# The begin of a decoder layer's kernel, rebuilt: S5 constants beside the input's arrival, S5 input tiles in pairs, another order of the halves

## The chip, the cores and the metric

The kernel runs on one core of one Trainium2 chip. The metric is the device time of one launch in microseconds, as the median of several runs. The engines are named as in the profile: PE (matrix multiplication; PEld is its weight load), DVE (VectorE), ACT (ScalarE), POOL (GpSimd) and SP (which here issues DMAs only).

## The reference, cut to what matters

One layer of a hybrid decoder on x (1024 tokens, 1024 channels), in float32. What the change touches is the first norm, the columns of the input projection that feed the S5 branch, and the numbers that the S5 branch derives from its parameters.

```python
h = rms_norm(x, norm_mix_pre[l])
proj = h @ w_in[l]                       # columns: RWKV-7 | S5 input u | two gates
u_s5 = proj[..., N_RWKV_COLS:N_RWKV_COLS + S5_WIDTH]      # 512 columns
...
lam = lax.complex(a_re, a_im)
dt = jnp.exp(log_step)[:, None]
a_bar = jnp.exp(lam * dt)
b_bar = ((a_bar - 1.0) / lam)[..., None] * lax.complex(b_re, b_im)
bu = jnp.einsum('gpc,blgc->blgp', b_bar, ug)
_, states = lax.associative_scan(s5_combine, (a_elems, bu), axis=1)
y = jnp.real(jnp.einsum('gcp,blgp->blgc', c, states)) + d * ug
```

RWKV-7 time mixing, the two gates, the output projection and a gated MLP follow.

## The kernel before, in words

Channels lie on the partitions, tokens along the free dimension, in two halves of 512 tokens. Each matmul operand is split into a high part, which ACT rounds to the matmul's format, and a low part, the rest, which DVE (for x: DVE and POOL in turn) subtracts. A product of two such operands is three matmuls (`mm3_steps`: high by high, low by high, high by low), so a tile of 128 columns by 512 tokens over the 8 blocks of 128 channels is 24 matmuls into one PSUM bank (`gm`).

The begin, up to the first tile of `mix_in` (the RWKV columns of the projection):

- `load_x` loads eight x tiles of a half. `setup` loads the constants (`csts`: an identity, masks, a row of numbers) and small vectors (`vecs`), and makes a few derived vectors on DVE.
- `norm` squares x on ACT, adds pairs on DVE, sums over channels with small matmuls on PE (`sumsq`, into `chk`), makes the reciprocal root with small dependent DVE instructions (`rstd`), spreads it over the partitions with PE (`spread`), copies that to SBUF (`rbc`), multiplies each x tile with it on DVE and splits the result into `hh` and `hl`.
- `s5_in` makes the four tiles of S5 input. Its weights come through `load_w`: an SP load into `wf` (two buffers), high part `wh` on ACT, low part `wl` on DVE (four buffers each). It takes tiles 0 and 1 over both halves, then 2 and 3; each result goes to DRAM (`US`) and comes back reordered (`u8`).
- `s5_setup` makes the S5 constants from the parameters: some 115 DVE instructions on 128 x 32 numbers, with sines on ACT.
- From then on two lanes run for each of four batches of eight S5 groups: `s5_tables` (tables on DVE, sines on ACT) and `s5_batch` (the rotation, the scan and the output).

PE's instructions stand in the order in which the code emits them. On the other engines a scheduler orders them by the priority under which they were emitted (`HPN` above `HPW` above `HP`). The emission order comes from `drive`: lanes yield their costs and due times, and between them work is taken from the list `self.fill`. In the kernel before, S5 input tiles are such fill work, half 1's norm is a lane, and `s5_setup` is emitted behind it at the lower priority `HP`:

```python
self.fill = [self.s5_in((0, 1)), self.s5_in((2, 3)), self.mix_in()] + ...
self.drive([(HPN, self.norm(1, xs[1], xp))])
with tc.high_priority(HP):
    self.s5_setup()
```

## Time and profile before

| | us |
|---|---|
| median of 3 runs (1638.65 to 1644.3) | 1640.43 |
| profiled execution | 1641.32 |
| its span, first to last instruction | 1639.5 |
| PE busy, of the span | 1513.2 (92%) |
| DVE busy | 1161.2 (71%) |
| ACT busy | 718.6 (44%) |
| POOL busy | 177.9 (11%) |
| first matmul of the S5 input tiles | 26.14 |
| first eviction of mix_in | 102.57 |

The profiled execution is one run; the difference between its time and its span lies around the first and the last instruction. Matmuls overlap, so a row shows 0.39 us for one that starts 0.23 us after the one before; start to start is what counts. A row of a timeline gives the start, the busy time, engine, line, operation, output and inputs, and in brackets the idle time before and what ended it. The granted clock of TensorE is 1.00 at full speed.

### The profile page before, as it was taken

What the parts mean: (1) busy time and instruction counts of PE and PEld (TensorE: products, weight loads), DVE (VectorE), ACT (ScalarE), POOL (GpSimd) and SP (SyncE); (2) the same over time, 40 slices, a digit from 0 to 9 for tenths busy, and PEclk for the clock granted to TensorE, in tenths of its full rate; (3) what the DMA queues carried; (4) which work ended last, traced back from release to release, by engine and by line L of the source; (5) the groups of instructions that cost most, each with busy time, mean ns of one, the idle gap of its engine ahead of it and who ended that gap; (6) DMA issues with size and microseconds to landing.
All of it is one profiled execution on the core that took longest, in us unless ns stands there. A gap on an engine that the chain in (4) does not pass through costs nothing. (4 is left out here: it accounts for less than half of the span.)

```text
span 1639.5 us, 23417 instructions
## 1 busy us (share of the span) xinstructions
PE 1513.2 (92%) x8644; PEld 1206.2 (74%) x8644; DVE 1161.2 (71%) x2091; ACT 718.6 (44%) x1173; POOL 177.9 (11%) x260
## 2 busy tenths in 40 slices
PE   5899898999997997989987999999999999999995
PEld 4688787777675775656765778778888888788774
DVE  5898765657544578586478478977777777778767
ACT  4345543222353344346543444544445445443451
POOL 2100102232112024212020000000000000000000
PEclk9799999999997998999999999999999999999997
DMA  5255243443333166444256254322222224862622
GB/s 176 68 146 158 85 129 116 141 127 100 103 105 109 63 184 186 117 118 153 85 153 229 88 193 145 131 90 78 90 78 77 92 89 152 295 227 93 227 92 103
DMA packets 115811, 212.67 MB, mean 130 GB/s; under 512 B 22208, under 2 KB 28352, under 8 KB 115696
## 3 DMA queue, kind: packets, MB, share of 16 engines
q1 hardware_dynamic: 102672, 174.16, 33.5%
q0 software_dynamic: 11296, 32.82, 6.8%
q10 hardware_dynamic: 1728, 4.20, 0.7%
q8 instruction: 68, 1.11, 0.3%
q14 instruction: 47, 0.39, 0.1%
HBM read 156.07 MB, written 52.95 MB: 127 GB/s over the span
## 5 line engine op out<-in xcount | busy, mean ns | idle before, releaser
L173 PE MATMUL gm<-hh,wh 128*128 128x512 f32 x688 | 300.1, 436 | 21.7 <-DVE last L966 7.2
L174 PE MATMUL gm<-hl,wh 128*128 128x512 f32 x688 | 280.1, 407 | 7.7 <-DVE hl L228 4.7
L175 PE MATMUL gm<-hh,wl 128*128 128x512 f32 x688 | 277.6, 404 | 0.0
L158 DVE TENSOR_TENSOR wl<-wf,wh 128x512 fp32r<-128x512 f32 x179 | 125.1, 700 | 106.5 <-ACT wh L157 103.9
L157 ACT CAST wh<-wf 128x512 fp32r<-128x512 f32 x179 | 110.7, 619 | 185.2 <-PE gm L174 96.0
L173 PEld LDWEIGHTS gm<-hh,wh 128*128 128x128 f32 x688 | 134.3, 195 | 58.8 <-issue 10.3
L174 PEld LDWEIGHTS gm<-hl,wh 128*128 128x128 f32 x688 | 134.9, 196 | 36.1 <-DVE hl L228 8.2
L175 PEld LDWEIGHTS gm<-hh,wl 128*128 128x128 f32 x688 | 134.9, 196 | 29.5
L1562 PE MATMUL d<-xl,wh 128*128 128x512 f32 x308 | 120.3, 391 | 4.1 <-DVE xl L228 4.1
L1561 PE MATMUL d<-xh,wh 128*128 128x512 f32 x308 | 120.2, 390 | 2.0 <-DVE zg L1417 2.0
L1563 PE MATMUL d<-xh,wl 128*128 128x512 f32 x308 | 119.9, 389 | 0.0
L1387 PE MATMUL rp<-t,h 128*128 128x512 f32 x216 | 84.4, 391 | 2.4 <-ACT p L1401 1.7
L1389 PE MATMUL rp<-t,l 128*128 128x512 f32 x216 | 84.2, 390 | 0.5 <-DVE l L228 0.5
L1388 PE MATMUL rp<-t,h 128*128 128x512 f32 x216 | 84.1, 389 | 0.0
L1562 PEld LDWEIGHTS d<-xl,wh 128*128 128x128 f32 x308 | 57.8, 188 | 17.7 <-DVE xl L228 5.8
L1561 PEld LDWEIGHTS d<-xh,wh 128*128 128x128 f32 x308 | 57.8, 188 | 14.4 <-DVE zg L1417 2.4
L1563 PEld LDWEIGHTS d<-xh,wl 128*128 128x128 f32 x308 | 57.8, 188 | 11.8
L227 ACT CAST h<-r 128x1024 fp32r<-128x1024 f32 x34 | 35.8, 1054 | 61.1 <-PE rp L1388 29.6
L228 DVE TENSOR_TENSOR l<-r,h 128x1024 fp32r<-128x1024 f32 x34 | 41.6, 1225 | 29.3 <-ACT h L227 27.7
L1408 DVE SCALAR_TENSOR_TENSOR y<-zv,vecs,y 128x1023 f32<-128x1023 f32 (+1 forms) x36 | 46.1, 1281 | 8.6 <-ACT y L1406 8.6
L1387 PEld LDWEIGHTS rp<-t,h 128*128 128x128 f32 x216 | 40.5, 188 | 11.9 <-ACT p L1401 2.5
L1389 PEld LDWEIGHTS rp<-t,l 128*128 128x128 f32 x216 | 40.5, 188 | 9.5 <-DVE l L228 1.0
(450 smaller groups left out, 3408.9 us busy)
## 6 DMA issues: line engine op xcount, KB each, us to landing
r<-in_w_up_dram SPq DMA_DIRECT2D x36, 512.0 KB, 3.9
wf<-in_w_in_dram SPq DMA_DIRECT2D x68, 256.0 KB, 3.1
st<-in_w_down_dram SPq DMA_DIRECT2D x55, 256.0 KB, 4.3
st<-ACT SPq DMA_DIRECT2D x44, 256.0 KB, 4.5
wf<-in_w_up_dram SPq DMA_DIRECT2D x36, 256.0 KB, 2.9
ACT<-y POOLq DMA_DIRECT2D x18, 512.0 KB, 2.9
GT<-ev SPq DMA_DIRECT2D x32, 256.0 KB, 2.4
wf<-in_w_br_dram SPq DMA_DIRECT2D x32, 256.0 KB, 2.8
```

The lines of the kernel that those rows point to most:

```text
L157: nc.scalar.copy(h[:, :n], f[:, :n])
L158: nc.vector.tensor_tensor(l[:, :n], f[:, :n], h[:, :n].bitcast(F32), ALU.subtract)
L173: mm(ps, a, xh[k], start=k == 0, stop=False)
L174: mm(ps, a, xl[k], start=False, stop=False)
L175: mm(ps, b, xh[k], start=False, stop=k == n - 1)
L1387: mm(ps, wh[:, c], xh, start=first and k == 0, stop=False, skip_group_check=True)
L1388: mm(ps, wh[:, c], xl, start=False, stop=False, skip_group_check=True)
L1389: mm(ps, wl[:, c], xh, start=False, stop=k == 3, skip_group_check=True)
L1408: V.scalar_tensor_tensor(y[:, lag:], z[:, 0:1024 - lag], self.vec(nme, i), y[:, lag:], ALU.mult, ALU.add)
L1561: mm(ps, wh[:, c], xh[:, x], start=start, stop=False, skip_group_check=True)
L1562: mm(ps, wh[:, c], xl[:, x], start=False, stop=False, skip_group_check=True)
L1563: mm(ps, wl[:, c], xh[:, x], start=False, stop=stop, skip_group_check=True)
```

## The change

All of it lies ahead of `mix_in`.

- `setup` loads only the identity of `csts`. The other 608 KB are loaded on SP behind x, and so are the S5 parameters b and c of the first two batches. The three small S5 parameters that `s5_setup` begins with are loaded on ACT's queue instead of SP's.
- A new function `start` writes the order out by hand. `s5_setup` is emitted right behind half 0's norm, at a priority just under the norm's (`HPN - 50000`).
- `s5_in` takes two tiles at once: for each block of channels three matmuls of one tile and then three of the other. The order is tiles 2 and 3 of half 0, tiles 0 and 1 of half 0 (with half 1's norm between the steps), tiles 0 and 1 of half 1, and, as fill work, tiles 2 and 3 of half 1 (`s5_rest`). The weights of tiles 2 and 3 are loaded and split twice.
- In `norm`, all low parts are on DVE; the spread is read from PSUM, without the copy to SBUF; squares have eight buffers instead of four.
- `T_TAB0`, the due time of the first tables behind their start, is 18 instead of 38.

```diff
-        nc.gpsimd.dma_start(self.csts[:, 128:NCST], self.a["cst"][:, 128:NCST])
...
-            nc.sync.dma_start(ls, a["s5_ls"])
-            nc.sync.dma_start(lr, a["s5_a"][0])
-            nc.sync.dma_start(li, a["s5_a"][1])
+            nc.scalar.dma_start(ls, a["s5_ls"])
+            nc.scalar.dma_start(lr, a["s5_a"][0])
+            nc.scalar.dma_start(li, a["s5_a"][1])
...
-        self.spread(bc, self.rstd(ss, 1e-6, 1.0 / D))
-        rbc = pool.tile([128, 512], F32, tag="rbc", name=self.nm("rbc"), bufs=1)
-        nc.scalar.copy(rbc, bc)
+        self.spread(bc, y)
         h = []
         for k in range(NK):
-            nc.vector.scalar_tensor_tensor(xs[k], xs[k], self.vec("g_mix_pre", k), rbc, ALU.mult, ALU.mult)
-            h.append(self.hsplit(xs[k], k, self.hp[th], eng=nc.gpsimd if k % 2 else nc.vector))
+            nc.vector.scalar_tensor_tensor(xs[k], xs[k], self.vec("g_mix_pre", k), bc, ALU.mult, ALU.mult)
+            h.append(self.hsplit(xs[k], k, self.hp[th]))
...
-    def s5_in(self, bs):
...
+    def s5_in(self, bs, th, ws):
+
+        xh, xl = [h[0] for h in self.h[th]], [h[1] for h in self.h[th]]
+        ps = [self.gmp() for _ in bs]
+        for _ in zip(*(self.mm3_steps(p, w, 0, xh, xl) for p, w in zip(ps, ws))):
+            yield 1.36
+        for b, p in zip(bs, ps):
+            y = self.ev((128, 8, 64))
+            self.nc.scalar.copy(y.rearrange("p i n -> p n i"), p.rearrange("p (n j) -> p n j", j=8)[:, :, ::-1])
+            self.nc.sync.dma_start(self.US[b].rearrange("i c g n -> (c g) i n")[:, :, th * 64:th * 64 + 64], y)
...
+    def start(self, xp):
...
+        with tc.high_priority(HPN):
+            xs = [self.load_x(0, xp)]
+            self.setup()
+            norms = [self.norm(0, xs[0], xp)]
+        with tc.high_priority(HPW):
+            ws = [self.s5_ws((2, 3))]
+        go(norms[0], 6)
+        with tc.high_priority(HPW):
+            xs.append(self.load_x(1, xp))
+            norms.append(self.norm(1, xs[1], xp))
+        with tc.high_priority(HPN - 50000):
+            self.s5_setup()
+        with tc.high_priority(HP):
+            self.nc.sync.dma_start(self.csts[:, 128:NCST], self.a["cst"][:, 128:NCST])
+            self.s5w = {}
+            self.s5_load(0)
+            self.s5_load(1)
+        a = self.s5_in((2, 3), 0, ws[0])
+        go(a, 8)
+        with tc.high_priority(HPW):
+            ws.append(self.s5_ws((0, 1)))
+        go(a)
+        b = self.s5_in((0, 1), 0, ws[1])
+        go(b)
+        for _ in range(4):
+            go(norms[1])
+            go(b)
+        go(norms[1])
+        go(b, 1)
+        go(norms[1])
+        go(b, 3)
+        c = self.s5_in((0, 1), 1, ws[1])
+        go(c, 9)
+        for b in range(2):
+            self.load_u8(b)
+
+    def s5_rest(self):
+
+        yield from self.s5_in((2, 3), 1, self.s5_ws((2, 3)))
+        yield 0
+        self.load_u8(2)
+        self.stored = 3
...
-T_US, T_TAB0, T_TAB, T_TRIG, T_SCAN = 5.0, 38.0, 20.0, 12.0, 13.0
+T_US, T_TAB0, T_TAB, T_TRIG, T_SCAN = 5.0, 18.0, 20.0, 12.0, 13.0
```

The scheduler moves more than the diff tells. On DVE, half 0's reciprocal root (`rv` is the scaled sum of squares, `rsy` and `rsh` the steps of the root) was a run of its own before:

```order
L266 TENSOR_SCALAR rv_279<-chk_241 128x4
L137 TENSOR_SCALAR rsy_281<-rv_279 128x4
L138 TENSOR_SCALAR rsy_281<-rsy_281 128x4
L140 TENSOR_TENSOR rsh_282<-rsy_281 128x4
L141 SCALAR_TENSOR_TENSOR rsh_282<-rsh_282,rv_279 128x4
```

With the change, S5 constants (`sm`) stand between its steps, two after each:

```order
L266 TENSOR_SCALAR rv_285<-chk_248 128x4
L333 SCALAR_TENSOR_TENSOR sm_432<-sm_430,sm_422 128x32
L333 SCALAR_TENSOR_TENSOR sm_472<-sm_460,sm_470 128x32
L137 TENSOR_SCALAR rsy_287<-rv_285 128x4
L333 SCALAR_TENSOR_TENSOR sm_434<-sm_432,sm_422 128x32
L328 TENSOR_TENSOR sm_474<-sm_466,sm_472 128x32
L138 TENSOR_SCALAR rsy_287<-rsy_287 128x4
```

From the first step to the last these are 34 instructions, where 12 stood. On PE, half 1's sums of squares (`chk` from `ones` and `sq`) stood within the first two tiles of half 0, before:

```order
L175 MATMUL gm_381<-hh_321,wl_364 128x512
L246 MATMUL chk_356<-ones_205,sq_397 128x1 x4
L173 MATMUL gm_381<-hh_326,wh_363 128x512
L174 MATMUL gm_381<-hl_327,wh_363 128x512
L175 MATMUL gm_381<-hh_326,wl_364 128x512
```

Now they stand in the second pair (tiles 0 and 1, `gm_724` and `gm_725`), after each of its first four blocks of channels, and none is in the first pair:

```order
L175 MATMUL gm_724<-hh_306,wl_695 128x512
L173 MATMUL gm_725<-hh_306,wh_706 128x512
L174 MATMUL gm_725<-hl_307,wh_706 128x512
L175 MATMUL gm_725<-hh_306,wl_707 128x512
L246 MATMUL chk_732<-ones_204,sq_733 128x1 x4
L173 MATMUL gm_724<-hh_311,wh_694 128x512
```

Each block has six large matmuls where three stood. On ACT, the high parts of half 0 (`hh`) share the queue with half 1's squares (`sq_764` and so on) and the next weights (`wh`), now:

```order
L227 CAST hh_306<-x_184 128x512
L941 ACTIVATE sq_764<-x_355 128x512
L941 ACTIVATE sq_778<-x_357 128x512
L227 CAST hh_311<-x_186 128x512
L941 ACTIVATE sq_779<-x_359 128x512
L227 CAST hh_316<-x_188 128x512
```

Five of half 1's eight squares stand ahead of the first high part; before, none did. Behind the begin, PE's order is that of before, except that the matmuls of the S5 batches stand six places earlier among the projection's; from the end of the S5 batches on it is the same.

More of the change, by code (lines that the diff above doesn't have):

```diff
@@ L938, in norm @@
         ss = self.chk()[:, 0:512]
[L939 removed]
         for k in range(0, NK, 2):
[L941 removed]
+            sq = [pool.tile([128, 512], F32, tag="sq", name=self.nm("sq"), bufs=8) for _ in range(2)]
             for i in range(2):
@@ new lines, in s5_ws, with go @@
+    def s5_ws(self, bs):
+        return [self.load_w(self.a["w_in"][14 + b]) for b in bs]
+    def start(self, xp):
+        tc = self.tc
+        def go(gen, n=1):
+            for _ in range(n):
+                with tc.high_priority(HPN if gen in norms else HPW):
+                    next(gen, None)
+        with tc.high_priority(HPN):
[33 more added lines that the diff above has]
+            self.load_u8(b)
```

35 lines of the change are left out of this document (5 added, 30 removed).

## The prediction

> **What bounds the kernel now.** I read the page's busy slices first (40 slices of 41 us), then a table by stage, then PE's waits in the first 80 us.
>
> ```profile
> PE   5899898999997997989987999999999999999995
> PEclk9799999999997998999999999999999999999997
> ```
>
> PE is busy for 90% or more in most slices, so PE sets the time, and a stage is worth what PE loses in it. It loses most in the first slices, where the granted clock falls too.
>
> ```profile
> 0.00:26.14 26.14, 9.20 (x41) 8.77 (x41) 9.37 (x30) 9.99 (x16) 2.31 (x12) 1.00 0.84 255
> 38.00:47.80 9.80, 9.79 (x32) 8.44 (x33) 4.78 (x28) 1.06 (x1) 1.09 (x1) 0.50 0.11 28
> 58.40:68.50 10.10, 7.08 (x16) 5.11 (x17) 9.56 (x18) 3.27 (x6) 4.59 (x4) 0.50 0.17 49
> 178.20:192.00 13.80, 9.05 (x49) 7.91 (x49) 13.14 (x22) 4.05 (x6) 0.62 (x1) 0.75 0.29 86
> PE gm L174 <- DVE hl L228: 4.4, 5, 2.3
> PE gm L173 <- ACT hh L227: 4.3, 4, 2.1
> ```
>
> The first four rows are stages (length, busy time of PE, PEld, DVE, ACT and POOL with counts, granted clock, DMA share, GB/s). Some 20 us of the first 70 run at half clock, and PE waits 8.7 us for low and high parts of the normalised x (total, times, longest). The S5 input tiles are 4 tiles x 2 halves x 8 x 3 = 192 matmuls. These rows price one, and bound the stage:
>
> ```profile
> 91.43 0.39 PE L173 MATMUL gm<-hh,wh 128*128 128x512 f32 x1
> 96.87 0.39 PE L173 MATMUL gm<-hh,wh 128*128 128x512 f32 x1
> 34.45 0.95 PE L246 MATMUL chk<-ones,sq 128*128 128x1 f32 x8
> 39.03 1.70 PE L246 MATMUL chk<-ones,sq 128*128 128x1 f32 x8
> 26.14 0.80 PE L173 MATMUL gm<-hh,wh 128*128 128x512 f32 x1 [2.11 <-ACT hh L227]
> 31.23 0.40 PE L173 MATMUL gm<-hh,wh 128*128 128x512 f32 x1
> 102.57 0.69 ACT L963 ACTIVATE ev<-gm,mu 128x512 f32<-128x512 f32 x1 [2.29 <-PE gm L175]
> ```
>
> 24 matmuls lie between the first two: 5.44/24 = 0.227 us each at full clock. The eviction at 102.57 is mix_in's first, so its 24 matmuls began at 96.9. From 26.1 to 96.9 PE spent 70.7 us on 192 x 0.227 + 4 x 0.95 (square sums of half 1) + 1.1 (their spread, half of the 2.08 below) = 48.5 us of work at full clock. So 22 us are the most to be had here.
>
> **The change, step by step.** Times are us from the span's start.
>
> ```profile
> 3.62 0.62 ACT L157 CAST wh<-wf 128x512 fp32r<-128x512 f32 x1 [1.60 <-DMA wf<-in_w_in_dram]
> 9.11 0.93 SPq L156 DMA_DIRECT2D wf<-in_w_in_dram  x2
> 16.46 0.69 DVE L944 TENSOR_TENSOR sq<-sq,sq 128x512 f32<-128x512 f32 x1 [0.57 <-ACT sq L943]
> 19.11 3.76 SPq L931 DMA_DIRECT2D x<-in_x_dram  x8
> 19.55 0.16 DVE L266 TENSOR_SCALAR rv<-chk 128x4 f32<-128x4 f32 x1 [2.40 <-PE chk L246]
> 21.95 2.08 PE L272 MATMUL chk<-csts,rsy 128*128 128x128 f32 x8 [2.43 <-DVE rsy L142]
> 24.68 2.08 DVE L953 SCALAR_TENSOR_TENSOR x<-x,vecs,rbc 128x512 f32<-128x512 f32 x3 [2.79 <-ACT rbc L950]
> 66.86 0.18 DVE L329 TENSOR_TENSOR sm<-sm 128x32 f32<-128x32 f32 x1
> 66.96 0.18 DVE L329 TENSOR_TENSOR sm<-sm,sm 128x32 f32<-128x32 f32 x1
> 152.85 0.34 ACTq L618 DMA_DIRECT2D YU<-t  x1
> ```
>
> *Until x is normalised.* SP's third weight load waits for VectorE's first low weight part (9.11), and the last three x tiles of half 0 stand behind it in SP's queue. Twelve S5 instructions more now come ahead of that part, 0.10 apart as at 66.86: 1.3 later. Against that the 608 KB of constants leave the front, 2.4 us at 255 GB/s. I take the last square sum where it is, at 16.46 (-1.1 to +1.3). From 19.55 on, 34 VectorE instructions stand where 12 make the reciprocal root now: 34 x 0.105 = 3.6 instead of 2.3, +1.2. The copy of the spread (24.03 to 24.68) goes: -0.6. The half's first product starts at 25.2 instead of 24.7. The three tiny loads cost ACT's queue 3 x 0.34 = 1.0 ahead of its table load; its idle 1.60 before 3.62 hides that, without it 1.0 would be lost. Five squares of half 1 are queued on ACT ahead of the first high part at 25.9: their x no longer waits behind eight S5 loads, so it is issued from about 15.7 instead of 19.11 and is there. The S5 loads and constants behind it are wanted from 66 on: nothing.
>
> *Low parts on VectorE.* Groups by form in the first 80 us, and one product where POOL is idle:
>
> ```profile
> L953 DVE SCALAR_TENSOR_TENSOR x<-x,vecs,rbc 128x512 f32<-128x512 f32 x16 | 15.4, 999 | 2.8 <-ACT rbc L950 2.8
> L228 POOL TENSOR_TENSOR hl<-x,hh 128x512 fp32r<-128x512 f32 x8 | 11.6, 1461 | 53.9 <-ACT hh L227 53.9
> L228 DVE TENSOR_TENSOR hl<-x,hh 128x512 fp32r<-128x512 f32 x8 | 7.1, 901 | 1.1 <-ACT hh L227 1.1
> 32.47 0.74 DVE L953 SCALAR_TENSOR_TENSOR x<-x,vecs,rbc 128x512 f32<-128x512 f32 x1
> ```
>
> A product is 0.74 at 32.47 and 999 ns in the mean; a low part is 901, and the same form 0.69 at 16.46. Without POOL I take 0.66 and 0.60 from start to start (0.08 of each overlaps the next, as at 66.86). For the first half VectorE then does 8 products, 8 low parts, 3 square sums and 2 low weight parts: 8 x 0.66 + 13 x 0.60 = 13.1, and the last low part is done at 38.4. That a product reads PSUM is new here: bounds 0.66 and the mean of 999 ns, +2.7 for the half; a shifted tile's product from PSUM is 0.74 at 104.33 (below), so I take 0.66.
>
> *Half 0, tiles 2 and 3 abreast.* Six matmuls per k, 1.36 at full clock, against 1.3 to 1.6 of VectorE: PE is fed. It starts at 26.6, runs at half clock until about 31 (the first 0.40 is at 31.23 now) and ends the 48 matmuls at 40.4; now 24 are done by 39.03. *Half 0, tiles 0 and 1*: their second low weight part has 18 S5 instructions ahead of it and comes at 42.1; then 43 x 0.227 + 4 x 0.95 + 1.1 = 14.6, end 56.7. *Half 1, tiles 0 and 1*: products from 54.0 (12 matmuls before 56.7); 8 x 0.66 + 10 x 0.60 = 11.3, and 0.9 for high parts behind two evictions on ACT: 66.2, PE ends at 68.4. *Tiles 2 and 3*, whose weights are loaded again (four casts and four low parts more, behind PE's matmuls): 48 x 0.227 = 10.9. Mix_in begins at 79.3 instead of 96.9: **-17.6**.
>
> *The S5 lane.* From here PE's order is the old one, but S5's matmuls stand six places earlier (1.4 us). What counts is whether VectorE keeps up.
>
> ```profile
> 76.81 0.29 DVE L509 TENSOR_TENSOR sml<-s_b,s5q 128x128 f32<-128x128 f32 x1
> 104.33 0.74 DVE L964 SCALAR_TENSOR_TENSOR ev<-gm,vecs,ev 128x511 f32<-128x511 f32 x1
> 131.13 1.23 DVE L601 TENSOR_TENSOR t<-chk,t 128x1024 f32<-128x1024 f32 x1 [3.25 <-ACT t L579]
> 140.56 1.21 DVE L609 TENSOR_TENSOR t<-t,t 128x1024 f32<-128x1024 f32 x1
> 145.11 0.39 PE L614 MATMUL chk<-u,t 128*128 128x128 f32 x2
> 174.02 1.23 DVE L601 TENSOR_TENSOR t<-chk,t 128x1024 f32<-128x1024 f32 x1 [6.70 <-ACT t L579]
> 178.52 1.91 PE L554 MATMUL chk<-ca,sml 128*16 128x128 f32 x16 [0.28 <-DVE t L602]
> 184.90 0.79 PE L614 MATMUL chk<-u,t 128*128 128x128 f32 x2 [3.58 <-ACT wT L547]
> 186.58 0.77 PE L615 MATMUL chk<-t,ca 128*128 128x128 f32 x2 [0.89 <-DVE t L609]
> 227.09 0.46 PE L615 MATMUL chk<-t,ca 128*128 128x128 f32 x2 [2.22 <-DVE t L609]
> ```
>
> The tables start at 66.2 instead of 76.81: -10.6. With less idle time in between, the first scan's product comes at 118 (131.13: -13), and its states at 129 (141.8 now). PE would be there at 145.3 - 17.6 - 1.4 = 126.3 and waits 2.8. Batch 1: VectorE now idles 6.70 before 174.02, while ACT loads three tables ahead of the last sine; the new order has one there; states come at 166, PE at 165, a wait of 0.8 instead of 3.58 + 0.28 + 0.89, and no half clock (now 13.80 at 0.75, 3.4 lost). Batch 2: 0.6 instead of 2.22. Together 4.2 - (4.8 + 3.4 + 2.2) = -6. That hangs on small differences between two long queues. I book a quarter, **-1.5**, and keep -6, and +4 (each of three waits bringing its own 3.4 at half clock: 4.2 + 10.2 - 10.4), for the range. Behind the S5 lane the order is the same: 0.
>
> Sum: -17.6 - 1.5 = -19.1. The profiled execution took 1641.3 (span 1639.5), which gives 1622.2; the median of the runs is 0.9 lower: **1621**.
>
> **The rivals.** *The clock stays low.* From 38.00 to 47.80 PE was busy for 9.79 of 9.80 us and still at 0.50: there, groups of six matmuls alternated with square sums. The new second stage (42 to 57) has that pattern. At half clock its seven k after the stall take 1.36 longer each and the four sums 0.75: up to +12.5, while a spell of 9.8 us as now costs 4.9. I price it between, at +8: 1629. For it speaks that row; against it, that the low spell began after VectorE had starved PE, which two tiles abreast avoid. (The Trainium skill, "TensorE: Matmul & The Clock Gate", section "Part 1: The HAM clock gate", says that about 3.4 us of sustained matmul activity releases the clock. By that rule the stage runs fast and the sum holds; the row at 38.00 speaks against it, if busy time is activity.)
>
> *The gain is handed back.* PE's later waits end on VectorE, or on loads that may not move forward with PE; the next stage opens on such a load:
>
> ```profile
> 275.67 1.23 DVE L675 TENSOR_TENSOR_SCAN ld<-csts,ld 128x512 f32<-128x512 f32 x1 [3.90 <-DMA ld<-TZ]
> ```
>
> If the S5 lane frees its buffers as late as now, nothing is left: 1640; if only the 4.6 by which the lane lags behind PE (17.6 - 13) is lost, 1626. For it: that lag. Against: these loads follow mix_in's stores, which PE times.
>
> *Slower.* VectorE takes over eight low parts from POOL and four repeated ones, 7.2 us, and the S5 lane becomes the bound. If its states came 5 us behind PE in each of four batches, PE would lose 5 + 3.4 (half clock) each time: 33.6 against 17.6 + 10.4, +5.6: 1646. It decides at a wait of 3.6 in every batch; I find 2.8 in one and under 1 in two. *The change doesn't do what it says*: the S5 constants would still run after 27. The order leaves four in ten there, and the sum above has them; no case of its own.
>
> **How the numbers follow.** Forecast 0.62, low clock 0.17, handed back 0.13 (a third of it still faster), slower 0.08. Less than 0.3%, 4.9 us, can't be told from no change. Faster: 0.62 + 0.17 + 0.04 = 0.83; same 0.09; slower 0.08. The range goes from 1614 (the whole -6 and the earlier x) to 1636 (low clock, +4 and the slow PSUM product); the forecast's own is 1615 to 1628.
>
> **What would show it.** First product near 25.2, then 0.74 each, none of POOL's low parts; tile pairs ending near 40, 57, 68 and 79; clock near 1 from 32 on; mix_in's first eviction at 85 instead of 102.57; waits under 3 us at S5's last matmuls. It is wrong if the clock is 0.5 between 42 and 57, if a high part waits for half 1's squares, or if mix_in's lead has shrunk again by 290.

## The result, and the profile after

The changed kernel takes 1626.51 us (median; 1625.85 to 1627.63) where the kernel before takes 1639.54 in the same comparison: a ratio of 0.9904, with a 95% interval of 0.9881 to 0.9926. The medians lie 13.0 us apart, the two profiled executions (spans 1639.5 and 1624.7) 14.8; 0.0096 of 1639.54 would be 15.7. So the gain is known only to some 4 us, as the interval says. The forecast was 1621, with 1614 to 1636 as its range.

First the busy slices of the changed kernel's page, 40 slices of 41 us:

```profile
PE   5998998999989997899978999999999999999995
PEclk9999999999998997999988999999999999999997
```

PE's second slice went from 8 to 9 and its clock there from 7 to 9; the rest looks alike. The same as a table by stage (length; busy us of PE, PEld, DVE, ACT, POOL with counts; granted clock; DMA share; GB/s), of the kernel before:

```profile
0.00:25.00 25.00, 9.20 (x40) 8.76 (x40) 8.23 (x28) 9.32 (x14) 2.31 (x12) 1.00 0.83 249
25.00:57.00 32.00, 24.96 (x89) 18.30 (x89) 25.44 (x103) 14.04 (x25) 6.08 (x4) 0.84 0.12 39
57.00:110.00 53.00, 49.75 (x212) 39.83 (x213) 49.05 (x118) 21.83 (x33) 6.46 (x6) 0.90 0.46 129
110.00:130.00 20.00, 20.00 (x106) 17.16 (x105) 17.81 (x27) 11.33 (x17) 3.59 (x5) 1.00 0.49 142
```

and of the changed kernel:

```profile
0.00:25.00 25.00, 7.96 (x36) 7.82 (x37) 15.21 (x104) 13.17 (x23) 1.78 (x11) 1.00 0.75 243
25.00:57.00 32.00, 29.87 (x135) 23.99 (x135) 25.48 (x88) 11.74 (x22) 0.84 (x1) 1.00 0.28 85
57.00:110.00 53.00, 52.92 (x245) 42.83 (x245) 51.81 (x87) 28.23 (x41) 10.76 (x3) 1.00 0.49 141
110.00:130.00 20.00, 16.43 (x79) 13.32 (x79) 11.21 (x16) 11.33 (x14) 6.38 (x8) 0.92 0.50 158
```

Two things changed up to 110 us. PE is fed and at full clock (135 instead of 89 matmul records in 25 to 57). And VectorE has done 104 instead of 28 instructions while x arrives, so that it has 92.5 us of work behind it at 110 instead of 82.7. The rows from 110 to 130 show what comes then: PE, which was busy for all of that stretch before (20.00), is now busy for 16.43 of it: it waits. Its longest wait there is for an eviction on ACT:

```profile
126.51 0.67 PE L173 MATMUL gm<-lx,wh 128*128 128x512 f32 x1 [3.07 <-ACT ev L996]
```

The front itself, from the changed kernel's timeline (start, length, engine, line, operation; in brackets the idle time before it and what ended it):

```profile
18.27 0.69 DVE L942 TENSOR_TENSOR sq<-sq,sq 128x512 f32<-128x512 f32 x1
24.16 2.07 PE L272 MATMUL chk<-csts,rsy 128*128 128x128 f32 x8 [3.23 <-DVE rsy L142]
26.27 0.75 DVE L951 SCALAR_TENSOR_TENSOR x<-x,vecs,chk 128x512 f32<-128x512 f32 x1 [0.94 <-PE chk L272]
27.72 0.80 PE L173 MATMUL gm<-hh,wh 128*128 128x512 f32 x1 [1.49 <-ACT hh L227]
44.51 0.95 PE L246 MATMUL chk<-ones,sq 128*128 128x1 f32 x8
86.90 0.69 ACT L960 ACTIVATE ev<-gm,mu 128x512 f32<-128x512 f32 x1 [3.29 <-PE gm L175]
```

Mix_in's first eviction is at 86.90 instead of 102.57, 15.7 earlier. Behind it I follow the S5 lane by four marks: its first matmuls on PE (the transposes, L545 before and L544 now), the first and the last output batch, and the first rotation of the RWKV stage. The kernel before:

```profile
105.72 0.49 PE L545 MATMUL chk<-csts,t 128*128 128x128 f32 x3
145.34 0.39 PE L615 MATMUL chk<-t,ca 128*128 128x128 f32 x2
261.28 0.39 PE L615 MATMUL chk<-t,ca 128*128 128x128 f32 x2
324.44 0.83 PE L705 MATMUL rp<-ar,bk 64*128 64x128 f32 x10
```

The changed kernel, with the lane's first scan product (on VectorE) between:

```profile
88.75 0.49 PE L544 MATMUL chk<-csts,t 128*128 128x128 f32 x3
124.49 1.22 DVE L600 TENSOR_TENSOR t<-chk,t 128x1024 f32<-128x1024 f32 x1 [5.11 <-ACT t L578]
135.88 0.46 PE L614 MATMUL chk<-t,ca 128*128 128x128 f32 x2 [1.62 <-DVE t L608]
247.81 0.39 PE L614 MATMUL chk<-t,ca 128*128 128x128 f32 x2
312.16 0.49 PE L704 MATMUL rp<-ar,bk 64*128 64x128 f32 x4
```

PE reaches the transposes 17.0 earlier, but the first output batch is only 9.5 earlier, the last 13.5 and the RWKV stage 12.3. So the lead of the front isn't handed on whole: the lane keeps a pace of its own. Which of the parts made the gain was the question for the chip.

### The profile page after: what moved, and what is told of

Same layout as the page of the kernel before. It is cut to its first block, busy times and chain, and to the rows that moved or that the text cites. A ratio compares the mean times of both kernels' runs of the same rounds, so it can differ in the third digit from the quotient of the medians.

```text
span 1624.7 us, 23434 instructions
## 1 busy us (share of the span) xinstructions
PE 1505.0 (93%) x8644; PEld 1200.3 (74%) x8644; DVE 1157.2 (71%) x2103; ACT 717.6 (44%) x1173; POOL 175.9 (11%) x251
## 5 line engine op out<-in xcount | busy, mean ns | idle before, releaser
L158 DVE TENSOR_TENSOR wl<-wf,wh 128x512 fp32r<-128x512 f32 x183 | 127.9, 700 | 115.1 <-ACT wh L157 113.4
L1447 ACT COPY p<-rp 128x512 f32<-128x512 f32 x54 | 31.1, 575 | 37.2 <-PE rp L1435 37.2
```

The costliest lines, as they stand in the source:

```text
L158: nc.vector.tensor_tensor(l[:, :n], f[:, :n], h[:, :n].bitcast(F32), ALU.subtract)
```

## The experiments

Each run has six or twelve executions, and is compared with the kernel before on the same chip. The prediction's theory is **front**: the time follows PE's start of mix_in. Against it stands **lane**: the time follows the S5 lane, and PE's tiles are fill.

**The changed kernel again**, as a control: the same code.

> The changed kernel once more, unchanged, beside the three experiments of this call. The first measurement gave 1626.5 us and a ratio of 0.9904. The four kernels that were run between gave ratios of 0.9929 to 0.9988, on a chip whose runs of the kernel before spread from 1635 to 1648. If that spread is the chip's, this ratio is 0.991 to 0.994 and the time 1628 to 1632 us there; if the four edits cost what they showed, it is 0.989 to 0.991 again.

Measured: 1626.11 us, 0.9905 (0.9884 to 0.9926). So the runs made beside it (one tile at a time, low parts on POOL, 128 bytes more) can be held against 0.9905; the others ran at other times, most on another chip, beside the kernel before but without this control. Its profiled execution has mix_in's first eviction at 85.29, the first output batch at 134.18 and the last at 248.24, up to 1.7 from the first profile's: one profile's landmarks are good to some 2 us.

**Two abreast, undone.**

```diff
-        for _ in zip(*(self.mm3_steps(p, w, 0, xh, xl) for p, w in zip(ps, ws))):
-            yield 1.36
+        for n, (p, w) in enumerate(zip(ps, ws)):
+            for i, _ in enumerate(self.mm3_steps(p, w, 0, xh, xl)):
+                if i % 2:
+                    yield 1.36
```

> The changed kernel with the S5 input tiles one after the other within each pair, instead of two abreast: this one part undone; halves, weights and evictions stand as they are. Theory (two abreast gives PE 1.36 us of work for each block of x, about what ACT and VectorE need to make one, so that PE neither waits nor drops its clock): one tile alone has 0.68 us of work for a block that takes 1.26 to 1.4, PE waits about 0.6 for each of 7 blocks in both halves' first tile, the first pair ends 2 to 5 us later than 42, the second half's first pair likewise, the clock falls below full in 26 to 70, and mix_in's first eviction is at 90 to 96 instead of 86.90 (ratio 3 to 5 thousandths above the changed kernel's). Rival (the order of the halves and the early squares did it): the eviction within 1.5 us of 86.90.

Measured: 1626.63 us, 0.9910 (0.9886 to 0.9933). ACT's first eviction of mix_in and PE's first output batch in its timeline:

```profile
92.17 0.69 ACT L960 ACTIVATE ev<-gm,mu 128x512 f32<-128x512 f32 x1 [2.54 <-PE gm L175]
134.60 0.46 PE L614 MATMUL chk<-t,ca 128*128 128x128 f32 x2 [0.81 <-DVE t L608]
```

The first half of the expectation held (mix_in 5.3 later than in the first profile, 6.9 than in the control; the clock stayed at 1.00, which it should not have), and the time did not follow: the batches come as in the changed kernel, and the ratio is 0.0005 from the control's, where 5.3 us are 0.0032. Five microseconds of the front cost nothing that shows. That speaks against the front theory, and in favour of the lane.

**Low parts on POOL again.**

```diff
-            h.append(self.hsplit(xs[k], k, self.hp[th]))
+            h.append(self.hsplit(xs[k], k, self.hp[th], eng=nc.gpsimd if k % 2 else nc.vector))
```

> The changed kernel with the low parts of odd blocks of x on POOL again, in both norms: this one part undone. Theory (VectorE alone is quick enough, and without POOL's reads beside it a product takes 0.74 instead of 1.0 us): a product takes 0.85 to 1.0 in the mean again, POOL's low part 1.3 to 1.6, and mix_in's first eviction comes 0.5 to 3 us after 86.90. Rival (VectorE sets the pace, and POOL takes work from it): the eviction 0.5 to 2 us before 86.90. Either way L998's stall at 99 to 112 stays if it is VectorE's instructions with two SBUF inputs that block POOL, though POOL has run eight instructions before.

Measured: 1627.02 us, 0.9904 (0.9881 to 0.9926); mix_in's first eviction at 87.65, first output batch at 133.88. This part is worth nothing that shows either. Its groups by form in the first 80 us (busy us, mean ns):

```profile
L951 DVE SCALAR_TENSOR_TENSOR x<-x,vecs,chk 128x512 f32<-128x512 f32 x16 | 11.4, 740 | 2.4 <-PE chk L272 2.4
L228 POOL TENSOR_TENSOR hl<-x,hh 128x512 fp32r<-128x512 f32 x8 | 11.6, 1444 | 51.7 <-ACT hh L227 51.7
```

POOL's low parts are there as before the change (1444 ns, 1461 then), and yet a product takes 740 ns and not 999. In the kernel before it read x and the copied spread, both from SBUF; now it reads the spread from PSUM. The single products bear that out: before, the four that lay beside a POOL low part took 1.75 to 1.77 and the other twelve 0.74 or 0.75; here eight lie beside one, wholly or in part, and all take 0.73 to 0.75. So the old 999 was the price of two SBUF inputs beside POOL, and the dropped copy took it away, not the move of the low parts.

**S5 constants at low priority.** Where they are emitted did not change, only the priority.

```diff
-        with tc.high_priority(HPN - 50000):
-            self.s5_setup()
         with tc.high_priority(HP):
+            self.s5_setup()
             self.nc.sync.dma_start(self.csts[:, 128:NCST], self.a["cst"][:, 128:NCST])
```

> The changed kernel with the S5 constants emitted at the low priority that they had before, in the same place of the code: this one part undone. VectorE then has nothing of S5 ahead of the low weight parts and square sums: the last square sum is at 16.5 to 17 (as before) and the reciprocal root takes 2.0 to 2.4 instead of 3.2, so mix_in's first eviction is at 84.5 to 85.5 instead of 86.90. The constants then run in VectorE's gaps behind the norms, and the S5 lane begins later. If the early constants are worth what the prediction booked (the lane being covered by fill), the time is within 1.5 us of the changed kernel's, at either side; if the lane sets the time in the S5 stage, it is 2 to 6 us above it (ratio 0.992 to 0.994).

Measured: 1632.03 us, 0.9933 (0.9917 to 0.9949), which overlaps the control's interval, on another chip. It was no real undoing: the scheduler still put S5 instructions wherever VectorE was free, 94 VectorE instructions in the first 25 us instead of 104. The last square sum came at 17.76, the root took longer (5.08 instead of 3.23), mix_in's first eviction came at 87.89 and the first batch at 136.75. Inconclusive, so the loads had to be moved too:

**S5 parameters loaded late**, the part undone for good.

```diff
-            nc.scalar.dma_start(ls, a["s5_ls"])
+            nc.sync.dma_start(ls, a["s5_ls"])
 (and the same for the two others; s5_setup at priority HP as above)
```

> The changed kernel with the three loads of the S5 parameters on SP behind half 1's x (as the kernel before had them) and the constants emitted at the low priority HP, so that VectorE cannot make them while x arrives: this part really undone (the run with only the priority lowered left 94 of 104 VectorE instructions in the first 25 us). Everything else of the change stays. Theory 'lane' (from about 57 us VectorE's work for the S5 tables sets the time; the tiles of PE are fill, so the front's gain on PE counts for little): the last square sum comes at 16.5 to 17.2 and mix_in's first eviction within 2 us of 86.90, yet the first S5 output batch is at 139 to 146 instead of 135.88 and the last at 252 to 258 instead of 247.81, and the time is 4 to 9 us above the changed kernel's 1626 (ratio 0.993 to 0.996). Theory 'front' (the prediction's sum: PE's earlier start of mix_in is the gain): the time follows mix_in's first eviction, within 1.5 us of the changed kernel's (ratio 0.989 to 0.9915).

Measured: 1633.15 us, 0.9968 (0.9949 to 0.9987). VectorE's first stage, mix_in's first eviction and the first output batch:

```profile
0.00:25.00 25.00, 9.99 (x41) 9.05 (x41) 10.87 (x32) 12.87 (x20) 1.78 (x11) 1.00 0.81 260
84.08 0.69 ACT L960 ACTIVATE ev<-gm,mu 128x512 f32<-128x512 f32 x1 [1.72 <-PE gm L175]
145.79 0.55 PE L614 MATMUL chk<-t,ca 128*128 128x128 f32 x1 [8.90 <-DVE t L608]
```

This is the clearest run of the study. Without the S5 instructions (32 VectorE instructions in the first stage) mix_in is 2.8 earlier than in the changed kernel (1.2 than in the control), and the program is slower: 0.9968 - 0.9905 = 0.0063, some 10 us, though on another chip. On its own chip it can be held against the kernel with L998 on VectorE and the sines kept together (below, 0.9917): 0.0051, some 8 us. PE waits 8.90 for the lane, whose first batch is where it was before the change, and the last comes at 255.63. Front said "within 1.5 us" and falls. By the ratios two thirds of the gain hang on the early constants; the medians (1641.66 before, 1633.15 here) leave more of it, 8.5 us of the control's 14.8, and the twelve times fall into two groups (seven from 1632.1 to 1633.3, five from 1636.6 to 1640.6), so the share is rough.

**The constants early, alone**, in the kernel before.

```diff
                     xs = [self.load_x(0, xp)]
                     self.setup()
+                with tc.high_priority(HPN - 50000):
+                    self.s5_setup()
 (its three loads on ACT's queue; the later call of s5_setup goes)
```

> The kernel before with one part of the change alone: the S5 parameters loaded from ACT's queue and the S5 constants emitted early at high priority. Halves, tiles one at a time, low parts on POOL and constants' load stay as before, so mix_in's first eviction stays within 3 us of 102.57. Theory 'lane': VectorE has some 7 us of S5 work behind it by 25 us, the first output batch is at 136 to 141 instead of 145.34, and the time falls by 4 to 9 us (ratio 0.9945 to 0.9975). Theory 'front': nothing but the front's own small delay, ratio 0.999 to 1.001. If both parts are needed (the lane's matmuls then stand behind fill that PE has not yet done), the first output batch comes earlier but the last does not, and the ratio is 0.998 to 1.000.

Measured: 1641.56 us, 0.9994 (0.9976 to 1.0012). The lane theory alone falls here. A stage of its table, then PE's transposes, the VectorE instruction that waits for the matmuls behind them, and the first output batch:

```profile
57.00:110.00 53.00, 48.65 (x213) 38.38 (x214) 40.84 (x63) 21.56 (x29) 6.62 (x6) 0.97 0.43 129
105.62 0.60 PE L545 MATMUL chk<-csts,t 128*128 128x128 f32 x4
108.54 0.29 DVE L511 TENSOR_TENSOR sml<-sml,sml 128x128 f32<-128x128 f32 x1 [1.47 <-PE chk L554]
145.23 0.39 PE L615 MATMUL chk<-t,ca 128*128 128x128 f32 x2
```

VectorE had its S5 work done early, and then idled for 12 of the 53 us (40.84 busy): the transposes stand behind 231 matmuls of input tiles in PE's order (225 in the changed kernel), and PE got to them at 105.62, as before. The ratio is the one expected if both parts are needed, but the first batch did not come earlier, as that case had it. (In this kernel the scaled square sum came 7 us later, at 26.68 instead of 19.55, and mix_in still began as before, at 102.46: PE's half-clock spells were shorter, with a granted clock of 1.00 instead of 0.84 from 25 to 57 and 0.97 instead of 0.90 from 57 to 110.) So the lane has two feeders. Its first batch comes when VectorE has made the tables **and** PE has worked off the fill that stands ahead of the lane's matmuls.

**The constants early, and the lane sooner in PE's order.** One number more than in the run before:

```diff
-T_US, T_TAB0, T_TAB, T_TRIG, T_SCAN = 5.0, 38.0, 20.0, 12.0, 13.0
+T_US, T_TAB0, T_TAB, T_TRIG, T_SCAN = 5.0, 26.0, 20.0, 12.0, 13.0
```

> The kernel before with the S5 constants early, as in the run before, and the S5 lane's first due time T_TAB0 at 26 instead of 38, so that its first matmuls (the transposes of L545) stand behind 180 fill matmuls in PE's order instead of 231. With early constants alone VectorE was idle for 12 us between 57 and 110 and waited for these matmuls at 108.54, and the first output batch stayed at 145.23. Halves, single tiles and low parts on POOL stay as before: PE's half-clock spells of the front too. Theory 'two paths' (the S5 stage ends with the later of two: VectorE's path to the lane, and PE's fill ahead of the lane's matmuls; the change shortens both): the transposes come at 92 to 97, the first output batch at 132 to 138, the last at 249 to 255, and the time falls by 5 to 11 us (ratio 0.993 to 0.997). Rival 'front' (PE's lost time in the front is never made up): the batches come earlier but PE waits or works off the fill later; the first rotation of the RWKV stage stays within 2 us of 324.44 and the ratio is 0.998 to 1.001.

Measured: 1624.39 us (1617.7 to 1629.12), 0.9909 (0.9887 to 0.9931): the whole gain of the change, beyond what was expected, with the old front. The same marks, from a profiled execution that is the fastest of the six (1617.7):

```profile
94.86 0.38 PE L545 MATMUL chk<-csts,t 128*128 128x128 f32 x2
106.22 0.69 ACT L963 ACTIVATE ev<-gm,mu 128x512 f32<-128x512 f32 x1 [4.08 <-issue]
134.48 0.39 PE L615 MATMUL chk<-t,ca 128*128 128x128 f32 x2
310.28 0.38 PE L705 MATMUL rp<-ar,bk 64*128 64x128 f32 x2
```

Mix_in's first eviction is 3.7 *later* than before any change (the lane's matmuls now pass it), single tiles, POOL's low parts and the old order of the halves are all there, and the RWKV stage begins 14.2 earlier. These marks need care. All four batches stand 51 matmuls of tiles sooner in PE's order (180 instead of 231 ahead of the first transposes, 633 instead of 684 ahead of the last batch); 51 x 0.227 = 11.6 us, so the batches are earlier by the order alone. At the RWKV stage, where PE has 888 such matmuls behind it in the other kernels of the table, it has 864 here: a tile of 24, 5.4 us, is still to do, and 14.2 - 5.4 = 8.8 are gained. The rest of the gain comes later, and was not followed up.

What went are PE's later waits, for more fill is left when they come (one of 3.1 for an eviction came instead). Those of the kernel before up to 330 us (total, times, longest):

```profile
PE gm L173 <- DVE last L966: 7.2, 1, 7.2
PE chk L614 <- ACT wT L547: 3.6, 1, 3.6
```

The early constants alone left both as they are (7.2 and 3.6 there too). Here the first is 0.3, and the second has no row any more:

```profile
PE gm L173 <- DVE last L966: 0.3, 1, 0.3
```

The runs side by side (us; landmarks from the one profiled execution of each):

| kernel | mix_in's 1st eviction | lane's transposes | 1st output batch | last batch | RWKV's 1st rotation | ratio to before |
|---|---|---|---|---|---|---|
| before | 102.57 | 105.72 | 145.34 | 261.28 | 324.44 | 1 |
| changed | 86.90 | 88.75 | 135.88 | 247.81 | 312.16 | 0.9904 |
| changed, again | 85.29 | 87.14 | 134.18 | 248.24 | 311.43 | 0.9905 |
| one tile at a time | 92.17 | 94.01 | 134.60 | 247.06 | 311.70 | 0.9910 |
| parameters late | 84.08 | 85.93 | 145.79 | 255.63 | 318.88 | 0.9968 |
| before + early constants | 102.46 | 105.62 | 145.23 | 261.70 | 325.12 | 0.9994 |
| before + early constants + T_TAB0 26 | 106.22 | 94.86 | 134.48 | 249.36 | 310.28 | 0.9909 |

The ratio goes with the columns of the last batch and of the RWKV stage, and not with the column of mix_in. The first batch alone doesn't give it: with the parameters late it is where it was before, and part of the gain is left. Nor do these marks give the ratio to a thousandth: the runs with S5 constants at low priority and with x first (below), on another chip, have the last batch at 248.64 and 248.98, and both are at 0.9933. T_TAB0 alone, in the kernel before without the early constants, was not tried.

**POOL's stall.** In the changed kernel's timeline POOL's first two `tensor_scalar` on the evictions (L998) take 5.17 and 7.25 us; before, the same eight took 0.61 to 1.01. POOL's two, then three VectorE instructions of that time:

```profile
99.24 5.17 POOL L998 TENSOR_SCALAR ev<-ev 128x512 f32<-128x512 f32 x1 [49.99 <-DVE cb L537]
104.43 7.25 POOL L998 TENSOR_SCALAR ev<-ev 128x512 f32<-128x512 f32 x1
103.86 0.73 DVE L961 SCALAR_TENSOR_TENSOR ev<-gm,vecs,ev 128x511 f32<-128x511 f32 x1
104.58 1.20 DVE L521 TENSOR_TENSOR t<-sml,s5ar 128x1024 f32<-128x1024 f32 x1
110.53 0.67 DVE L158 TENSOR_TENSOR wl<-wf,wh 128x512 fp32r<-128x512 f32 x1
```

They were no longer preceded by POOL's low parts, so "cold" (code is fetched at first use) was one reading; the other was "blocked": the first ends 0.55 after VectorE's L961 begins, which reads PSUM, and the second about 0.5 after VectorE's unbroken row of instructions with two SBUF inputs, which begins with L521 and ends with L158 at 111.2. (From 99.24 to 103.86 VectorE's row has one instruction of another kind, a `tensor_scalar` with a single SBUF input at 102.12, 0.68 long, which ended nothing.) One tiny instruction of the same form was put early:

```diff
         nc.gpsimd.memset(self.hpi, math.pi / 2)
+        self.warm = self.const.tile([128, 32], F32, name="warm")
+        nc.gpsimd.memset(self.warm, 0.0)
+        nc.gpsimd.tensor_scalar(self.warm, self.warm, 1.0, 1.0, ALU.add, ALU.mult)
```

> The changed kernel with one more tiny POOL instruction (tensor_scalar on 128x32, the form of L998) in the first 15 us, so that L998 at 99 us is no longer the first of its kind. In the changed kernel L998's first two instructions take 5.17 and 7.25 us, the other six 0.61 to 0.78. Theory 'cold' (the first instructions of a kind are slow because POOL has to fetch their code): the two take 0.6 to 0.8, the waits for ev buffers at 106.55 and 113.84 go, the first scan product is at 119 to 120 instead of 124.49, and the time is 3 to 5 us below the changed kernel's 1626.5 (ratio to the kernel before about 0.988). Theory 'blocked' (POOL waits while VectorE runs instructions with two SBUF inputs back to back: the first ends 0.55 after VectorE's L961, which reads PSUM, begins at 103.86, the second 0.55 after VectorE's row of such instructions ends at 111.13): both stay within 0.5 us of 5.17 and 7.25, and the ratio stays at 0.990.

Measured: L998 (here L1001) about as slow as without it (the second 0.6 shorter), though the tiny one at 3.01 had taken 0.21:

```profile
99.25 5.06 POOL L1001 TENSOR_SCALAR ev<-ev 128x512 f32<-128x512 f32 x1 [50.12 <-ACT ev L999]
104.33 6.66 POOL L1001 TENSOR_SCALAR ev<-ev 128x512 f32<-128x512 f32 x1
```

And in the run with one tile at a time the first of its kind, without any early one, met VectorE at another moment:

```profile
104.06 0.62 POOL L998 TENSOR_SCALAR ev<-ev 128x512 f32<-128x512 f32 x1 [56.55 <-ACT ev L996]
```

(Its third stalled, for 5.97.) So cold is out. Blocked fits where these stalls end, but it is not shown, for two runs speak against it. With the low parts on POOL again, the eight took at most 1.39, though VectorE ran instructions with two SBUF inputs without a gap from 104.53 to 112.46:

```profile
104.97 1.39 POOL L998 TENSOR_SCALAR ev<-ev 128x512 f32<-128x512 f32 x1 [0.17 <-ACT ev L996]
```

That run's expectation said that the stall would stay. With the parameters late it was at most 1.39 beside a row from 103.35 to 112.25, and 2.12 in all. So such a row doesn't stall POOL by itself; what else it takes stays open. (The Trainium skill, "GPSIMD Engine Reference", section "2.1 Instruction dispatch", puts a first call to freshly loaded code at about 6 us; 0.62 for a first one does not show it here. "SBUF — State Buffer", section "SBUF: two separate sides", says that a VectorE instruction with two SBUF inputs and a GpSimd one exclude each other for the whole of an instruction. The ends of the stalls agree, but the stall outlasts many instructions: VectorE's were 0.27 to 1.21 long, and POOL did not get in between them for 6.6 us.) The total of this run, 1641.12 us and 0.9988 (0.9974 to 1.0002), was far off both expectations; the tile itself is tried below.

**L998 on VectorE**, to price the stall.

```diff
-                        nc.gpsimd.tensor_scalar(t, t, 1.0, 1.0, ALU.add, ALU.mult)
+                        nc.vector.tensor_scalar(t, t, 1.0, 1.0, ALU.add, ALU.mult)
```

> The changed kernel with L998's eight instructions on VectorE instead of POOL; nothing else. Both theories on POOL expect that the stall goes: L998 takes 0.35 to 0.7 each on VectorE (8 of them, 3 to 5 us of VectorE's time), the eviction at 113.84 comes 3 to 4 us earlier, the first scan product at 119 to 121 instead of 124.49. If the stall is what was given back between 87 and 200 us, the time falls by 2 to 4 us (ratio 0.988 to 0.989). If the gain was lost elsewhere (PE's later waits by 290 us come last anyway), the ratio stays at 0.990.

Measured: 1630.19 us, 0.9929 (0.9909 to 0.9949): no gain. An L998 took 0.41 on VectorE, and the sines' input was ready 2.5 earlier (L576, which takes its absolute value, at 116.90 instead of 119.41), but the scan product came at 124.83 instead of 124.49. ACT's timeline shows why:

```profile
117.98 1.28 ACT L577 ACT_TABLE_LOAD   x1
120.35 1.28 ACT L996 ACT_TABLE_LOAD   x1
122.35 1.28 ACT L578 ACT_TABLE_LOAD   x1
125.90 1.28 ACT L996 ACT_TABLE_LOAD   x1
```

A tanh (L996) now stands between the two sines (L577, L578) on ACT, and each of these changes between sine and tanh cost a load of 1.28. The first output batch came at 138.46. So the sines were also kept together:

```diff
+        with self.tc.high_priority(HPN):
             A.activation(cs, ph, AF.Abs)
             A.activation(sn, ph, AF.Sin, scale=SIN_SCALE)
             A.activation(cs, cs, AF.Sin, bias=self.hpi, scale=-SIN_SCALE)
```

> The changed kernel with L998 on VectorE, as in the run before, and the three activations of the S5 tables (absolute value, two sines) raised above the evictions in priority, so that no tanh stands between the two sines: no operation added. In the run with L998 on VectorE alone, the tables' input was ready 2.5 us earlier (115.64 instead of 118.15), but four ACT_TABLE_LOADs of 1.28 us stood between 117.98 and 127.18 where the changed kernel has two, and the first scan product came at 124.83. Theory (POOL's stall is worth 2.5 us to the lane, and the table loads took it back): two table loads, first scan product at 121.3 to 122.5, first output batch 131.5 to 134, time 2 to 4 us below the changed kernel's (ratio 0.9875 to 0.989). Rival (PE's fixed order and the fill set the time of the batches): first scan product earlier, but the output batches within 1 us of 135.88 and 247.81, ratio 0.990 to 0.991.

Measured: 1627.95 us, 0.9917 (0.9894 to 0.9940). Two loads, and the first scan product at 121.13, 3.4 earlier than in the changed kernel (1.7 than in the control); but the output batches are at 134.18 and 247.20, the control's to 1.1, and the ratio lies within its interval. The second scan product came at 125.38 (125.63 in the changed kernel), since VectorE's queue had work for the evictions ahead of it. The rival was right in what it said of the time (the first batch is 1.7 off the 135.88 that it named, as the control's is): the stall, however odd, costs nothing that shows.

**x first in SP's queue.** The four weight loads of the first pair go through POOL's queue, so that no x stands behind a weight.

```diff
-            ws = [self.s5_ws((2, 3))]
+            ws = [self.s5_ws((2, 3), self.nc.gpsimd)]
```

> The changed kernel with the four weight loads of the first S5 input pair issued from POOL's queue instead of SP's, so that no x tile stands behind the third weight load, which waits for VectorE. Theory (the 1.8 us by which the last square sum is late, 18.27 instead of 16.46, come from that wait): the last square sum at 16.5 to 16.9, the first matmul at 26.0 to 26.4 instead of 27.72, mix_in's first eviction at 85.2 to 85.6 instead of 86.90, the time 1 to 2 us lower (ratio about 0.9895). Rival (the bytes bound it: x, four weights and constants come at one rate whatever the queue): the last square sum within 0.5 of 18.27. Second rival (POOL issues them later than SP would): the first matmul waits for a low weight part instead.

Measured: 1631.9 us, 0.9933 (0.9917 to 0.9949). The last square sum came at 17.23 instead of 18.27, but the root took 4.08, then half 1's squares stood ahead of the first high part on ACT (a wait of 2.59): the first matmul came at 29.01 instead of 27.72, and mix_in's first eviction at 86.81. The control has its last square sum at 17.35 without this edit, so the 17.23 don't show that the theory of the wait is right; and the delay stood on VectorE and along ACT's queue in its place.

**128 bytes more.** The early POOL instruction had a tile of its own; here is the tile with its memset, without that instruction.

```diff
         nc.gpsimd.memset(self.hpi, math.pi / 2)
+        self.shift = self.const.tile([128, 32], F32, name="shift")
+        nc.gpsimd.memset(self.shift, 0.0)
```

> The changed kernel with 128 bytes more per partition among the constants (a tile of 128x32 that POOL fills with zeros and nobody reads), so that every SBUF tile that is allocated behind it lies 128 bytes further; no other instruction. The run with the early POOL instruction had such a tile, and its MLP matmuls stood 0.2305 us apart (217 in 50 us) where the changed kernel's stand 0.2247 (222.5 in 50 us), so that it lost 12 us between 1000 and 1400 us. Theory (the place of the tiles in SBUF does that): the same pace of 217 in 50 us here, and the time 8 to 14 us above the changed kernel's of this call. Rival (the extra POOL instruction or a state of the chip did it): 222 to 223 in 50 us, and the changed kernel's time.

Measured: 1642.44 us, 1.0006 (0.9988 to 1.0023). The MLP from 1100 to 1150, of the changed kernel and of this one (busy PE with the count of matmuls first):

```profile
1100.00:1150.00 50.00, 50.00 (x223) 41.40 (x221) 39.00 (x43) 25.06 (x30) 1.06 (x2) 1.00 0.25 84
```

```profile
1100.00:1150.00 50.00, 50.00 (x217) 40.54 (x216) 35.43 (x40) 23.76 (x29) 1.60 (x3) 1.00 0.21 74
```

PE is busy throughout at full clock in both, and each matmul is 50/217 - 50/223 = 6 ns longer. The place of the tiles in SBUF does it, as expected; 16 us on the whole program, more than the change itself gains. It is not the MLP alone: by the profiles this kernel is level with the control at the RWKV stage (310.88 and 311.43), 8.5 behind it by the control's 1036, and 16.4 behind by its 1385. (The kernel before and all runs without the tile have 222 or 223 from 1100 to 1150, so in that stage the other comparisons are free of it.)

## Why the prediction was right in its number, and where its steps failed

**The front**, step by step.

- Last square sum at 16.46 with a bound of +1.3: it was 18.27, outside, and 17.35 in the control, inside; so about 1 us of it varies from run to run. The S5 instructions ahead of the low weight part cost what was counted. SP's third weight load, which waits for that part, came 1.2 later than the 9.11 of before:

```profile
10.28 0.92 SPq L156 DMA_DIRECT2D wf<-in_w_in_dram  x2
```

  What the sum had wrong is the 2.4 us that the constants' loading was to bring. The last square sum came 7.0 behind the issue of the last three x tiles (6.1 in the control), where it was 6.4 before. Without the S5 instructions and their loads it came at 15.13.
- Reciprocal root +1.2: +0.8 (3.23 for 2.43). The first product was 26.27 (25.2 predicted), the first matmul 27.72 (26.6).
- The four pairs ended near 42.7, 58.2, 70.0 and 81.1 (their first evictions) against 40.4, 56.7, 68.4 and 79.3: late by 1.5 to 2.3, of which 1.1 was there at the start; in between nearly as worked out.
- A product from PSUM at 0.66 from start to start, against the bound of 0.999: right (742 ns in the mean, with 0.08 of overlap). The reason given, that POOL is gone, was not what did it; with POOL back it is 740, because the product reads PSUM.
- Full clock from 32 on: nearly right (matmuls take 0.63 up to 33.79 and 0.39 from 34.60, though the granted clock reads 1.00 from 26 on); the square sums in 40 to 57 run at 0.95 for eight, as at 34.45 before. The rival of the low clock did not come. But its reason, that two abreast feed PE, is not what decides: one at a time kept 1.00 too. What made and what ended the spell of 38 to 47.8 was not found.
- Mix_in 17.6 earlier: 15.7 (17.3 in the control).
- Of the signs of being wrong, none came: the clock was 1.00 from 42 to 57, the first high part waited for its product and not for squares, and at 312 the lead was 12.3 of 15.7.

**The step that failed** is the one that made the sum: "Mix_in begins at 79.3 instead of 96.9: -17.6", taken over whole into the end, with -1.5 for the S5 lane on top. The runs showed that mix_in's start is not on the path. It moved by +5.3 without any time lost, by -2.8 with 8 to 10 us lost, and by +3.7 against the kernel before (there the lane's matmuls pass it) with the whole gain by the ratio. In its place stand the S5 lane's batches, which need VectorE's tables and PE's place in the order together. That the number came within 5.5 us of the forecast is in part luck: in this kernel mix_in's lead and the gain at the end happen to be alike (15.7 and 14.8), and the runs just named part them. The front's PE time mattered only as one way to bring PE to the lane's matmuls sooner (88.75 for 105.72), and it brought more than needed: transposes at 94.0 do as well.

The lane's own term had the wrong sign: -1.5 was booked (worked out to -6), and the lead fell from 15.7 at mix_in's first eviction to 12.3 at the first rotation of the RWKV stage, where the same matmuls are done: +3.4. The states were wanted at 129 and were there at 135.7 (VectorE's L608 from 134.51). PE waited only 1.62 for them and not 2.8, since it was late itself: it was ready at 134.3, not at 126.3. What the sum put at nothing are PE's waits for evictions on that way, 0.50 at 121.10 and 3.07 at 126.51 (its row stands with the result). The tanh that it waited for stood on ACT behind the two sines of the tables and their two table loads (121.07 to 125.77), and from 126.5 to 130 the granted clock was 0.53. The waits in the second and the third batch were 1.92 and 2.23, and not 0.8 and 0.6. So -17.6 - 1.5 was booked, and by the last batch 13.5 were gained, 12.3 at the first rotation of the RWKV stage, and 14.8 at the end.

**Behind the S5 lane: 0** was roughly right: 12.3 became 14.8. Runs of the same code differ by as much there (the control's profile gained another 1.9 in that part), so I draw nothing from it.

**The rivals.** "The gain is handed back" named part of the true mechanism, PE's lead ending on waits for VectorE and for buffers, and priced it by a lag of 4.6; what was lost of the 15.7 up to the RWKV stage is 3.4. "Slower", the S5 lane as the bound, was right that the lane is the bound and wrong that VectorE's extra low parts would make it late: the early constants put 104 - 28 = 76 more instructions into VectorE's first 25 us. That the constants would partly run after 27 held too (the last of them, L474, ran at 49.65), and still enough of them ran before.

## What to carry to other kernels

When an engine is busy for most of a stretch, that does not make its time the time: ask what its queue is fill for, and look for the dependent lane whose marks (here the last output batch and the next stage's first matmul) move with the total. Test it by making the busy engine late; five microseconds that cost nothing say more than any sum. And a change in many parts can owe its gain to two of them, neither of which brings it alone: early constants alone gained nothing, and the changed kernel without them a third of it by the ratios. With the early constants, one number in the order did as much by the ratio as the whole new front; where it did so behind the begin stays open. When marks are compared, count what is still to do behind them.

## What was not expected of the hardware

- A POOL instruction of 0.6 us took 5 to 7 us in some of these kernels while VectorE ran instructions with SBUF inputs without a gap. In the changed kernel it ended about 0.5 after VectorE began one that reads PSUM, or fell idle. In two other kernels it took at most 1.39 beside such rows, so what decides is open.
- A VectorE product that reads one input from PSUM took 0.74 beside POOL's low parts; with both inputs in SBUF it took 1.75 to 1.77 there.
- Moving the SBUF tiles by 128 bytes made PE's matmuls in the MLP 6 ns longer (217 instead of 223 in 50 us, at the same granted clock of 1.00) and the program 16 us slower. Two kernels with that tile showed it, on two chips, with and without an instruction that uses it. Which operand's place does it was not tried. A comparison of two kernels should therefore look at the pace of a stage that neither touches.
- Whether the new front on top of the earlier lane would give more than either (1626.11 and 1624.39, with intervals that overlap) was not tried.
